# A decoder block on one core: the first modulation columns summed two at a time, the first loads reordered, the rotary tables ahead, and the combinations of h as a stream

## The chip, the cores and the metric

The kernel runs on one core of a Trainium2 chip. The time is the device time of one execution, in microseconds; the kernel before takes 2710.49 us, the median of three runs from 2708.99 to 2712.02. PE is the matrix engine, DVE the vector engine, ACT the scalar engine, POOL GpSimd and SP the engine that issues most loads.

## The reference

One decoder block: 2048 tokens, 1024 features, float32 throughout. The parts that the change touches:

```python
mod = c @ w_ada[l] + b_ada[l]
shift_m, scale_m, gate_m, shift_f, scale_f, gate_f = jnp.split(mod, 6, axis=-1)

h = modulate(rms_norm(x, g_pre_mix[l]), shift_m, scale_m)      # h * (1 + scale) + shift
proj = h @ w_in[l]
q_a, k_a, v_a, q_m, k_m, v_m, o_m, i_m, f_m, g_a, g_m = jnp.split(proj, split_points, axis=-1)

q_a = rope(q_a.reshape(B, S, N_Q_HEADS, HEAD_DIM), positions)   # sin and cos of positions * inv_freq
k_a = rope(k_a.reshape(B, S, N_KV_HEADS, HEAD_DIM), positions)
...
```

Behind it come sliding-window attention with sinks, a chunkwise mLSTM, a gated merge with its output projection, and a SwiGLU feed-forward part. The modulation `mod` is a vector of 6 x 1024 numbers, the same for all tokens: no projection can start before the shift and scale of its columns of h are known.

## The kernel before

Every float32 matrix is split into a rounded high half and the rest, a low half (`whi` and `wlo` for weights, `hi` and `lo` for h). A product is three matmuls into one sum: high by high, high by low, low by high. ACT rounds the high halves (L256, L259, L518) and a subtraction gives the low ones (L257 and L260 for weights, L521 for h).

Tokens go in four blocks of 512 (`TB`), two blocks to a super-block of 1024 (`T2`). Within one, the q, k, v and mLSTM v projections of the first block come first, then those of the second, then projections that use both blocks at once with fewer products: they need `hcT1` to `hcT4`, combinations of h's blocks. `hprep` makes h of one block: loads of x, sums of squares on ACT (L500), the reciprocal root on POOL (L475), the scaled rows, then for each of 8 columns k (128 features each) a transposition on PE (L209) and two activations with that column's scale and shift (L518 the rounded half, L520 the full value), and the low half (L521, on POOL in the first block, on DVE in the others). In the odd block it also makes the combinations (L534 to L537) as soon as columns k and k+4 are there. `hsums` then moves two of the combinations within memory and splits them (L551, L552).

The start. `ADA` cuts the first 1024 shift and the first 1024 scale columns of `w_ada` into four chunks of 256. `load_ada` brings one chunk, 2 MB in four loads of 512 KB (L129). `ada_first` multiplies the 8 row groups of a chunk by c and adds them up, shift and scale each in an accumulator of its own, 128x256 per operation (L426 the first, L428 the other seven), on DVE. The shift of chunk 0 is summed on PE instead (16 matmuls, L204, then a copy on ACT, L443). Matmuls with ones add over the partitions, and L448 to L450 write the columns of `sh1` and `s1` for two k at a time; `first_h` then steps `hprep` through these two columns. `rope_tables` (L631 to L679) reduces position times frequency to an angle in some 35 operations on DVE and takes sine and cosine on ACT. `program()` puts it before the fourth chunk.

The order on each engine comes from a planner: it simulates the program and picks what can be issued next, so that the place of an instruction in the text does not fix its place in an engine's queue, except where a call pins it (`tc.issue_after`, `tc.keep_in_program_order`). Streams (`spawn`) are stepped as the planned time of PE, `now`, passes their due time, which a generator yields as a delay (`L_HT`, `L_HS` and others, ns). Loads of weights go through `wpool`'s raw tiles: a load waits until both halves of what was in its buffer are made. The first raw tiles hold the q weights (`raw_rows`, L290), then k, v and the gates' (`raw_cols`), then the mLSTM v weights (L290 again).

Of the kernel before, what the change touches and what calls it, by code (L numbers as in the profile page):

```python
# [10 lines left out]
F32 = mybir.dt.float32  # L11
F32R = mybir.dt.float32r
I32 = mybir.dt.int32
# [6 lines left out]
P = 128  # L20
# [17 lines left out]

L_X, L_HT, L_HS = 16000.0, 1400.0, 1500.0
L_ROPE, L_ROPEK, L_QK, L_ATT2 = 5000.0, 2100.0, 1500.0, 3500.0  # L40
# [8 lines left out]

ADA = [(0, 256, (0,)), (256, 256, ()), (512, 256, ()), (768, 256, ())]  # L50
ADA_AHEAD = (1, 3, 4)

# [19 lines left out]
def decoder_block(ctx: ExitStack, tc: tile.TileContext, a: dict, out: bass.AP, dbg=None):  # L72
# [48 lines left out]
    def load_ada(c0, n):  # L121

        kn = 2048 // n
        raws = {0: [], 1: []}
        for k0 in range(0, KD, 4):
            for part in (0, 1):
                if k0 % kn == 0:
                    raws[part].append(big([kn, n]))
                nc.sync.dma_start(raws[part][-1][:, k0 % kn:k0 % kn + 4, :],  # L129
                                  w_ada[:, part * D + c0:part * D + c0 + n].rearrange("(p k) c -> p k c", k=KD)[:, k0:k0 + 4, :])  # L130
        return {part: [raws[part][k // kn][:, k % kn, :] for k in range(KD)] for part in (0, 1)}

    x_first = [load_x(x_d, big, 0)]

    stack = tm([P, P])
    V.memset(stack, 0.0)
    r0 = 0
    off = {}
    for name, v, n in (("b_ada", a["b_ada"].rearrange("o (t p) -> (o t) p", p=P), 48),
                       ("g_pre_mix", a["g_pre_mix"].rearrange("o (t p) -> (o t) p", p=P), 8),  # L140
                       ("g_pre_ffn", a["g_pre_ffn"].rearrange("o (t p) -> (o t) p", p=P), 8),
                       ("conv_w", a["conv_w"].rearrange("o j (t p) -> (o j t) p", p=P), 32),
                       ("conv_b", a["conv_b"].rearrange("o (t p) -> (o t) p", p=P), 8),
                       ("norm_w", a["mlstm_norm_w"].rearrange("o (t p) -> (o t) p", p=P), 4)):
        nc.sync.dma_start(stack[r0:r0 + n, :], v)
        off[name] = r0
        r0 += n
    x_first.append(load_x(x_d, big, 1))
    posi = tm([S // P, P], I32)
    nc.sync.dma_start(posi, a["positions"].rearrange("o (t p) -> (o t) p", p=P))  # L150
    c_sb = const.tile([P, KD], F32, name="c_sb")
    nc.sync.dma_start(c_sb, a["c"].rearrange("o (p k) -> (o p) k", k=KD))
# [127 lines left out]
    def raw_cols(w, nk, c0, n):  # L280
# [4 lines left out]
        return Raw(load)  # L285

    def raw_rows(w, k0, nk, c0):
        def load():
            t = raw_tile([nk, 512])
            nc.sync.dma_start(t, w[k0 * P:(k0 + nk) * P, c0:c0 + 512].rearrange("(k p) c -> p k c", p=P))  # L290
            return t
        return Raw(load)
# [136 lines left out]

    def ada_first(c0, n, raws, on_pe):  # L430

        t0, nt = c0 // P, n // P
        acc = [tm([P, n]) for _ in range(2)]
        pt = mix_tile()
        ps = {part: mix_tile() for part in on_pe}
        for k in range(KD):
            for part in (0, 1):
                if part in on_pe:
                    mm(ps[part][0:1, :n], c_sb[:, k:k + 1], raws[part][k], k == 0, k == KD - 1)
                else:  # L440
                    ada_terms(acc[part], raws[part][k].unsqueeze(1), k, 1)
        for part in on_pe:
            A.copy(acc[part][0:1, :], ps[part][0:1, :n])  # L443
        for part in (0, 1):
            r = 1 if part in on_pe else P
            for j in range(nt):
                mm(pt[:, part * 8 + j:part * 8 + j + 1], acc[part][:r, j * P:(j + 1) * P], ones[:r, 0:1], True, True)
        V.tensor_tensor(sh1[:, t0:t0 + nt], pt[:, :nt], col("b_ada", t0, nt), op=ALU.add)  # L448
        V.tensor_tensor(s1[:, t0:t0 + nt], pt[:, 8:8 + nt], b1[:, 8 + t0:8 + t0 + nt], op=ALU.add)
        V.tensor_tensor(s1[:, t0:t0 + nt], s1[:, t0:t0 + nt], col("g_pre_mix", t0, nt), op=ALU.mult)  # L450

# [34 lines left out]
    def hprep(b, first=False):  # L486
# [25 lines left out]
        def one(k):  # L512
            name = f"{k // 4 + 1}{odd + 1}"
            hi, lo = (hc_part(name, i)[:, k % 4, :] for i in range(2))
            ps = mix_tile()
            for t in range(NT):
                transpose(ps[:, t * P:(t + 1) * P], xs[t][:, k * P:(k + 1) * P])
            A.activation(hi, ps, AF.Identity, scale=s1[:, k:k + 1], bias=sh1[:, k:k + 1])  # L518
            v = vs[k // 4][:, k % 4, :]
            A.activation(v, ps, AF.Identity, scale=s1[:, k:k + 1], bias=sh1[:, k:k + 1])  # L520
            (G if first else V).tensor_tensor(lo, v, hi.bitcast(F32), op=ALU.subtract)  # L521

# [100 lines left out]
    NS = T2 // P  # L623

    def rope_tables(sb):

# [47 lines left out]
        V.tensor_scalar(y, y, -lim, lim, op0=ALU.max, op1=ALU.min)  # L674
        V.scalar_tensor_tensor(t2, y, -1.0, y, op0=ALU.mult, op1=ALU.min)
        sin = small.tile([P, NS, 32], F32, tag="sin", name=nm("sin"), bufs=1)
# [34 lines left out]
    def c_tile(n):  # L711
        C[n] = kvp.tile([P, MH, MD + 1], F32, tag="cst", name=nm("cst"), bufs=3)
        return C[n]

    hp0 = hprep(0, first=True)
    next(hp0)
    tables = {}

    def first_h(c0, n, on_pe):
        ada_first(c0, n, ada_raws[c0], on_pe)  # L720
        for _ in range(n // P):
            next(hp0)
# [13 lines left out]
    def superblock(sb):  # L736
# [1101 lines left out]
    phase2 = run2(program2())  # L1838
    for _ in run2(program(), {i: lambda i=i: ada_raws.update({c0: load_ada(c0, n) for c0, n, _ in ADA[ADA_AHEAD[i - 1]:ADA_AHEAD[i]]}) for i in (1, 2)}):
        pass  # L1840
# [29 lines left out]
```

## Time and profile before

| | |
|---|---|
| runs | 2708.99, 2710.49, 2712.02 us |
| the profiled execution's own time | 2716.59 us |
| its span, first to last instruction | 2714.9 us |
| mean granted clock of PE | 0.990 |
| HBM traffic over the span | 185 GB/s |
| low halves of the first h on POOL (L521) | 8, 1.45 us mean |
| chunk sums on DVE up to 62 us (L426, L428) | 56, 28.1 us busy |

The page gives busy times and shares for each engine; a group line gives the line of the code, the engine, the operation, what is written and read, how often, and the busy time, mean length and idle time before it with what ended that. A line of the timeline begins with the start in us from the span's start, and the length; `x4` means that four equal instructions run one behind another and overlap; in square brackets stands how long the engine had been idle and what it waited for. SPq is SP's queue, where the length is that of issuing a load and not of its transfer.

### The profile page before, as it was taken

The numbers are of one execution on the slowest core, as the hardware profiler recorded it, in microseconds if no ns is written. First come the engines' busy times: TensorE is split into PE (matmuls) and PEld (weight loads), VectorE is DVE, ScalarE is ACT, GpSimd is POOL, SyncE is SP. The second block draws the span as 40 slices with busy tenths as digits, with TensorE's granted clock in tenths as the row PEclk, the third lists the DMA queues.
The fourth block names the chain that finished last, engine by engine and source line by source line (L and its number), as shares of the span: only waits on it lengthen the run. The fifth ranks groups of instructions, "written<-read, shape, count | busy, mean of one in ns | idle before, by whom it ended". The sixth has DMA issues, their size and how long they took to land.

```text
span 2714.9 us, 35793 instructions
## 1 busy us (share of the span) xinstructions
PE 2639.2 (97%) x12310; PEld 2138.9 (79%) x12310; DVE 1986.2 (73%) x3906; ACT 1299.8 (48%) x2558; POOL 148.2 (5%) x189
## 2 busy tenths in 40 slices
PE   6989999999998999999999999999999999999998
PEld 4867788888885678888887888888877888888886
DVE  7968788778695778876687777776677676766456
ACT  5556544444755564444563443335554333333444
POOL 2010001100101000110000000000000000000000
PEclk8999999999998999999999999999999999999999
DMA  7654355897574544678765564436675232324566
GB/s 249 206 184 157 128 172 179 269 340 248 196 235 147 196 138 138 213 231 291 251 224 198 175 201 152 155 113 213 215 271 188 97 117 86 113 97 144 186 210 217
DMA packets 353639, 511.90 MB, mean 189 GB/s; under 512 B 25120, under 2 KB 213660, under 8 KB 348208
## 3 DMA queue, kind: packets, MB, share of 16 engines
q1 hardware_dynamic: 353456, 509.61, 56.9%
q8 instruction: 97, 1.59, 0.2%
q14 instruction: 86, 0.70, 0.1%
HBM read 357.12 MB, written 144.02 MB: 185 GB/s over the span
## 4 chain that ended last, share of the span: by engine, by line
PE 85%; DVE 7%; DMA 4%; ACT 2%; issue 1%; POOL 0%; SPq 0%; DVEq 0%; ACTq 0%; POOLq 0%
PE acc L204 61%; PE mix L204 22%; PE mix L209 2%; DVE hl L1357 1%; DVE tm L428 1%; DMA raw<-as_d 1%; ACT tm L946 1%; ACT hl L1356 1%; DMA raw<-in_w_in_dram 1%; DMA at_d<-tx 0%; DMA big<-in_x_dram 0%; DVE wlo L260 0%; DMA tx<-in_w_ada_dram 0%; DVE w L1667 0%; DMA at<-at_d 0%
## 5 line engine op out<-in xcount | busy, mean ns | idle before, releaser
L204 PE MATMUL acc<-big,hl 128*128 128x512 f32 x3936 | 940.8, 394 | 4.3 <-ACT tx L827 1.8
L204 PEld LDWEIGHTS acc<-big,hl 128*128 128x128 f32 x3936 | 733.3, 188 | 172.5 <-issue 13.8
L1356 ACT CAST hl<-raw 128x512 fp32r<-128x512 f32 x732 | 440.1, 621 | 493.4 <-PE acc L204 222.2
L1357 DVE TENSOR_TENSOR hl<-raw,hl 128x512 fp32r<-128x512 f32 x732 | 496.3, 694 | 194.8 <-ACT hl L1356 194.0
L204 PE MATMUL acc<-whi,big 128*128 128x512 f32 (+1 forms) x1280 | 379.3, 377 | 10.8 <-ACT big L518 8.4
L204 PEld LDWEIGHTS acc<-whi,big 128*128 128x128 f32 x1280 | 236.2, 192 | 52.4 <-ACT big L518 8.5
L204 PE MATMUL mix<-big,hl 128*128 128x512 f32 x1056 | 263.9, 391 | 1.7 <-ACT hl L1356 1.1
L204 PE MATMUL acc<-wlo,big 128*128 128x512 f32 (+1 forms) x640 | 241.2, 379 | 6.4 <-DVE wlo L260 6.4
L204 PE MATMUL acc<-hl,hl 128*128 128x512 f32 x1008 | 237.4, 393 | 5.1 <-DVE hl L1357 3.4
L204 PEld LDWEIGHTS mix<-big,hl 128*128 128x128 f32 x1056 | 197.9, 188 | 45.9 <-ACT hl L1356 1.9
L204 PEld LDWEIGHTS acc<-hl,hl 128*128 128x128 f32 x1008 | 187.0, 188 | 50.9 <-DVE hl L1357 8.8
L204 PE MATMUL mix<-hl,hl 128*128 128x512 f32 x792 | 182.7, 391 | 1.3 <-DVE hl L1357 0.9
L204 PEld LDWEIGHTS mix<-hl,hl 128*128 128x128 f32 x792 | 147.9, 188 | 35.3 <-DVE hl L1357 3.1
L204 PE MATMUL acc<-big,whi 128*128 128x512 f32 x512 | 157.4, 393 | 0.0
L260 DVE TENSOR_TENSOR wlo<-raw,whi 128x1024 fp32r<-128x1024 f32 (+1 forms) x96 | 109.0, 1137 | 65.5 <-ACT whi L259 59.8
L259 ACT CAST whi<-raw 128x1024 fp32r<-128x1024 f32 (+1 forms) x96 | 94.3, 983 | 123.8 <-PE acc L204 110.4
L204 PEld LDWEIGHTS acc<-wlo,big 128*128 128x128 f32 x640 | 123.7, 193 | 28.3 <-DVE wlo L260 8.6
L475 POOL TENSOR_TENSOR rs<-ms,nhalf 128x1 f32<-128x1 f32 (+1 forms) x56 | 42.6, 772 | 1617.5 <-DVE ms L473 1610.5
L204 PE MATMUL mix<-hcT4h,hl 128*128 128x512 f32 x352 | 117.7, 395 | 0.7 <-ACT hl L1356 0.7
L204 PE MATMUL acc<-hcT2h,hl 128*128 128x512 f32 x352 | 117.6, 394 | 0.0
L204 PEld LDWEIGHTS acc<-big,whi 128*128 128x128 f32 x512 | 95.4, 188 | 19.2
L204 PE MATMUL acc<-big,wlo 128*128 128x512 f32 x256 | 97.7, 393 | 0.0
(330 smaller groups left out, 3491.5 us busy)
## 6 DMA issues: line engine op xcount, KB each, us to landing
raw<-in_w_in_dram SPq DMA_DIRECT2D x48, 1024.0 KB
as_d<-w SPq DMA_DIRECT2D x154, 256.0 KB
raw<-as_d SPq DMA_DIRECT2D x70, 512.0 KB
raw<-in_w_ffn_gate_dram SPq DMA_DIRECT2D x22, 1024.0 KB
raw<-in_w_ffn_up_dram SPq DMA_DIRECT2D x22, 1024.0 KB
raw<-ws_d SPq DMA_DIRECT2D x40, 512.0 KB
y_d<-tm SPq DMA_DIRECT2D x64, 256.0 KB
tx<-in_w_ada_dram SPq DMA_DIRECT2D x64, 256.0 KB
```

The source lines that it names most:

```text
L204: T.matmul(o, lhsT=lhsT, rhs=rhs, start=start, stop=stop, skip_group_check=resumed)
L209: T.transpose(o, i, ident[:k, :k])
L259: A.copy(hv, src)
L260: V.tensor_tensor(lv, src, hv.bitcast(F32), op=ALU.subtract)
L428: V.scalar_tensor_tensor(acc, raw[:, k, :], c_, acc, op0=ALU.mult, op1=ALU.add)
L475: G.tensor_tensor(r[:, :n], ms[:, :n], nhalf[:, :n], op=ALU.pow)
L946: A.activation(sc[g][:, j, :], sc[g][:, j, :], AF.Exp, bias=nm_[:, hd:hd + 1], accum_out=sums[:, hd:hd + 1])
L1356: A.copy(v(hi), src)
L1357: V.tensor_tensor(v(lo), src, v(hi).bitcast(F32), op=ALU.subtract)
```

## The change

Six things change, all in the first phase:

- `load_ada` puts shift and scale of a chunk into one tile side by side, still in four loads. `ada_first` becomes `ada_half` (four of the eight row groups of a chunk; one operation of 128x512 sums both) and `ada_columns` (the matmuls with ones, and one operation for each column of `s1` and `sh1`, 16 and not 12 in all). Nothing of it is left on PE but the matmuls with ones. `first_h(i)` issues the first half of chunk i+1 ahead of the columns of chunk i, and its second half behind them.
- `last_sum` pins the first sum of each chunk behind the last sum of the chunk before; for chunk 0 behind the last operation of `rope_tables(0)`, which is called before the first chunk.
- First loads: x0, positions, c, x1, the first q weights, then the chunks (the loads of the first two q weights are kept in the program's order). The eight small vectors load through ACT's queue.
- The low halves of the first h (L521) are subtracted on DVE.
- The combinations leave `hprep` for a stream of their own, `hcombos`, with two steps for each k, spawned with a delay of 12000, which then goes on to `hsums` of T2 and T4.
- `ADA_AHEAD` becomes (0, 3, 4): none of the chunks is loaded ahead of the planned program.

```diff
-ADA = [(0, 256, (0,)), (256, 256, ()), (512, 256, ()), (768, 256, ())]
-ADA_AHEAD = (1, 3, 4)
+ADA = [(0, 256), (256, 256), (512, 256), (768, 256)]
+ADA_AHEAD = (0, 3, 4)
...
+        raws = []
+        src = w_ada[:, :2 * D].rearrange("(p k) (s c) -> p k s c", k=KD, s=2)
         for k0 in range(0, KD, 4):
+            raw = big([4, 2 * n]).rearrange("p k (s c) -> p k s c", s=2)
+            for s_ in range(2):
+                nc.sync.dma_start(raw[:, :, s_, :], src[:, k0:k0 + 4, s_, c0:c0 + n])
+            raws += [raw[:, k, :, :] for k in range(4)]
+        return raws
-    x_first = [load_x(x_d, big, 0)]
...
+    posi = tm([S // P, P], I32)
+    nc.sync.dma_start(posi, a["positions"].rearrange("o (t p) -> (o t) p", p=P))
+    x_first = [load_x(x_d, big, 0)]
+    c_sb = const.tile([P, KD], F32, name="c_sb")
+    nc.sync.dma_start(c_sb, a["c"].rearrange("o (p k) -> (o p) k", k=KD))
+    x_first.append(load_x(x_d, big, 1))
...
-        nc.sync.dma_start(stack[r0:r0 + n, :], v)
+        nc.scalar.dma_start(stack[r0:r0 + n, :], v)
...
-    nc.sync.dma_start(b_if, a["b_if"].to_broadcast([P, 8]))
+    nc.scalar.dma_start(b_if, a["b_if"].to_broadcast([P, 8]))
...
-    nc.sync.dma_start(sinks, a["attn_sinks"].to_broadcast([P, HQ]))
-    ada_raws = {c0: load_ada(c0, n) for c0, n, _ in ADA[:ADA_AHEAD[0]]}
+    nc.scalar.dma_start(sinks, a["attn_sinks"].to_broadcast([P, HQ]))
...
+            ins = nc.sync.dma_start(t, w[k0 * P:(k0 + nk) * P, c0:c0 + 512].rearrange("(k p) c -> p k c", p=P))
+            if first_rows:
+                tc.keep_in_program_order(ins)
+                first_rows.pop()
...
-    def ada_first(c0, n, raws, on_pe):
...
+    def ada_half(c0, n, raws, half):
+        if half == 0:
+            ada_acc[c0] = tm([P, 2, n])
+        acc = ada_acc[c0]
+        for k in range(4 * half, 4 * half + 4):
+            c_ = c_sb[:, k:k + 1]
+            if k == 0:
+                with tc.issue_after(last_sum[0].ins):
+                    last_sum[0] = V.tensor_scalar(acc, raws[k], c_, None, op0=ALU.mult)
+            else:
+                last_sum[0] = V.scalar_tensor_tensor(acc, raws[k], c_, acc, op0=ALU.mult, op1=ALU.add)
+                if k == 4:
+                    tc.keep_in_program_order(last_sum[0])
+
+    def ada_columns(c0, n):
         t0, nt = c0 // P, n // P
+        acc = ada_acc[c0]
         pt = mix_tile()
+        for part in (1, 0):
             for j in range(nt):
+                mm(pt[:, part * 8 + j:part * 8 + j + 1], acc[:, part, j * P:(j + 1) * P], ones[:, 0:1], True, True)
+        for j in range(nt):
+            t = t0 + j
+            V.scalar_tensor_tensor(s1[:, t:t + 1], pt[:, 8 + j:9 + j], b1[:, 8 + t:9 + t], col("g_pre_mix", t), op0=ALU.add, op1=ALU.mult)
+            V.tensor_tensor(sh1[:, t:t + 1], pt[:, j:j + 1], col("b_ada", t), op=ALU.add)
...
-            (G if first else V).tensor_tensor(lo, v, hi.bitcast(F32), op=ALU.subtract)
+            V.tensor_tensor(lo, v, hi.bitcast(F32), op=ALU.subtract)
...
+    def hcombos():
+        for k in range(4):
             t1, t2, t3, t4 = (HR[n][:, k, :] for n in ("T1", "T2", "T3", "T4"))
             V.tensor_tensor(t1, t3, t1, op=ALU.subtract)
             V.tensor_tensor(t3, t2, t3, op=ALU.subtract)
+            yield L_HS
             V.tensor_tensor(t2, t2, t1, op=ALU.subtract)
             V.tensor_tensor(t4, t4, t2, op=ALU.subtract)
-            yield L_HT
+            yield L_HS
+        yield from hsums(("T2", "T4"))
...
-        V.scalar_tensor_tensor(t2, y, -1.0, y, op0=ALU.mult, op1=ALU.min)
+        last_sum[0] = V.scalar_tensor_tensor(t2, y, -1.0, y, op0=ALU.mult, op1=ALU.min)
...
+    tables[0] = rope_tables(0)
+
+    def first_h(i):
+        def half(j, h):
+            if j < len(ADA):
+                ada_half(*ADA[j], ada_raws[ADA[j][0]], h)
+        if i == 0:
+            half(0, 0)
+            half(0, 1)
+        half(i + 1, 0)
+        ada_columns(*ADA[i])
+        half(i + 1, 1)
+        for _ in range(ADA[i][1] // P):
             next(hp0)
...
-        yield lambda: hps.update(t=spawn(hsums(("T2", "T4"))))
+        yield lambda: hps.update(t=spawn(hcombos(), L_HCB))
...
-        for i, ch in enumerate(ADA):
-            if i == 3:
-                yield lambda: tables.update({0: rope_tables(0)})
-            yield lambda ch=ch: first_h(*ch)
+        for i in range(len(ADA)):
+            yield lambda i=i: first_h(i)
```

More of the change, by code (lines that the diff above doesn't have):

```diff
@@ L428, in ada_terms @@
                 V.scalar_tensor_tensor(acc, raw[:, k, :], c_, acc, op0=ALU.mult, op1=ALU.add)
-    def ada_first(c0, n, raws, on_pe):
+    ada_acc = {}
+    def ada_half(c0, n, raws, half):
[12 more added lines that the diff above has]
+    def ada_columns(c0, n):
         t0, nt = c0 // P, n // P
-        acc = [tm([P, n]) for _ in range(2)]
+        acc = ada_acc[c0]
         pt = mix_tile()
[L435 to L445, printed above, removed]
-            for j in range(nt):
[L447 to L450, printed above, removed]
+        for part in (1, 0):
+            for j in range(nt):
+                mm(pt[:, part * 8 + j:part * 8 + j + 1], acc[:, part, j * P:(j + 1) * P], ones[:, 0:1], True, True)
[3 more added lines that the diff above has]
+            V.tensor_tensor(sh1[:, t:t + 1], pt[:, j:j + 1], col("b_ada", t), op=ALU.add)
     def ada_stream(parts, gap):
@@ L1838, in decoder_block @@
     phase2 = run2(program2())
[L1839 removed]
+    for _ in run2(program(), {i: lambda i=i: ada_raws.update({c0: load_ada(c0, n) for c0, n in ADA[ADA_AHEAD[i - 1]:ADA_AHEAD[i]]}) for i in (1, 2)}):
         pass
```

24 lines of the change are left out of this document (5 added, 19 removed).

## The prediction

> **What bounds the kernel now.** I read the page first, then a table of stretches with each engine's busy time, then the timeline of the first 80 us.
>
> ```profile
> span 2714.9 us, 35793 instructions
> PE 2639.2 (97%) x12310; PEld 2138.9 (79%) x12310; DVE 1986.2 (73%) x3906; ACT 1299.8 (48%) x2558; POOL 148.2 (5%) x189
> ...
> 0.00:20.00 20.00, 6.69 (x18) 2.13 (x18) 9.51 (x39) 10.50 (x21) 3.97 (x45) 1.00 0.79 281
> 20.00:40.00 20.00, 12.65 (x56) 10.18 (x56) 19.93 (x53) 6.59 (x12) 2.81 (x2) 0.81 1.08 388
> 40.00:60.00 20.00, 15.79 (x78) 13.16 (x79) 15.88 (x40) 11.40 (x18) 7.33 (x5) 0.85 0.36 126
> 60.00:80.00 20.00, 17.46 (x117) 15.40 (x117) 16.52 (x37) 16.44 (x37) 3.29 (x5) 1.00 0.23 79
> ...
> 100.00:120.00 20.00, 17.95 (x106) 16.02 (x106) 16.67 (x42) 11.15 (x22) 0.00 (x0) 0.94 0.91 301
> ...
> 160.00:180.00 20.00, 13.14 (x80) 8.03 (x79) 10.63 (x31) 13.11 (x48) 4.16 (x4) 0.89 0.43 138
> ...
> 200.00:740.00 540.00, 539.97 (x2595) 439.99 (x2594) 418.42 (x881) 294.15 (x591) 50.92 (x51) 1.00 0.65 213
> 740.00:1000.00 260.00, 240.01 (x1236) 182.36 (x1234) 200.62 (x506) 145.59 (x363) 17.52 (x17) 0.95 0.57 182
> ```
>
> Behind a stretch and its length come the busy us of PE, PE's weight loads, DVE, ACT and POOL, then granted clock, DMA share and GB/s. PE is busy 97% of the span and does not pause between 200 and 740 us, so a delay of PE's work before 200 us arrives at 740 us whole. PE is idle for 27.4 us of the first 80 (80 less 6.69, 12.65, 15.79, 17.46), 2.05 us in 100 to 120, 6.86 us in 160 to 180. From 20 to 40 us DVE is the full engine (19.93 of 20): PE waits for the modulation's sums.
>
> ```profile
> 6.03 0.63 ACT L500 ACTIVATE big<-big 128x512 f32<-128x512 f32 x1 [3.96 <-DMA big<-in_x_dram]
> 9.85 0.43 DVE L631 TENSOR_TENSOR tx<-inv_freq,pos 128x256 f32<-128x256 f32 x1
> 10.62 0.61 ACT L500 ACTIVATE big<-big 128x512 f32<-128x512 f32 x1
> ...
> 13.95 5.96 PE L204 MATMUL mix<-big,c_sb 128*1 128x256 f32 x16 [4.43 <-DMA big<-in_w_ada_dram]
> 15.33 0.35 DVE L426 TENSOR_SCALAR tm<-big,c_sb 128x256 f32<-128x256 f32 x1 [3.41 <-DMA big<-in_w_ada_dram]
> ...
> 25.26 0.15 DVE L450 TENSOR_TENSOR s<-s,cols 128x2 f32<-128x2 f32 x1
> 26.34 0.80 PE L204 MATMUL acc<-whi,big 128*128 128x512 f32 x1 [3.79 <-ACT big L518]
> 27.18 2.94 DVE L428 SCALAR_TENSOR_TENSOR tm<-big,c_sb,tm 128x256 f32<-128x256 f32 x2
> ...
> 35.20 1.67 DVE L428 SCALAR_TENSOR_TENSOR tm<-big,c_sb,tm 128x256 f32<-128x256 f32 x4
> 44.47 3.33 DVE L428 SCALAR_TENSOR_TENSOR tm<-big,c_sb,tm 128x256 f32<-128x256 f32 x3
> 52.09 0.42 DVE L675 SCALAR_TENSOR_TENSOR tx<-tx 128x256 f32<-128x256 f32 x1
> 54.90 0.16 DVE L450 TENSOR_TENSOR s<-s,cols 128x2 f32<-128x2 f32 x1
> ```
>
> The rotary table (L631 to L675) runs from 9.85 to 52.09, slipped between the modulation's sums, and for 3.41 us before 15.33 DVE has nothing but the coming of w_ada. The scale of chunk 0 is ready at 25.26, PE's first product follows at 26.34, and the scale of chunk 3 is ready at 54.90.
>
> **The change part by part.** The built program's order shows the rest alike: PE's order differs only in about the first 300 us and in a stretch of super-block 1 near 740 to 1000 us.
>
> *First loads.* The eight small loads leave SP's queue for ACT's, and stand there ahead of ACT's table load and first Squares. There are eight completion lanes for the two queues together: ACT's sixth load waits for the landing of positions, which SP issues right behind x0, and its last for that of c.
>
> ```profile
> 1.29 0.45 SPq L145 DMA_DIRECT2D tm<-in_b_ada_dram  x1
> 0.79 1.28 ACT L500 ACT_TABLE_LOAD   x1 [0.79 <-PEq L1860]
> 7.79 3.15 SPq L129 DMA_DIRECT2D big<-in_w_ada_dram  x4
> ```
>
> An issue takes some 0.45 us. x0 was there at 6.03; two or three issues after that (about 1.2 us) and the table load (1.28 us, formerly hidden behind x0's coming) put the first Square at about 8.5. Eight Squares took from 6.03 to 11.4 (the last starts at 10.62, with 0.8 to its reading); without the wait for x1 they take 5.0, to 13.5. The sum of squares stands ahead of the rotary table in DVE's order, so the table begins at about 13.9 instead of 9.85: +4.05. Bounds: 11.5, if ACT isn't held at all (the Squares then end as before), and 14.5. w_ada comes some 3 us sooner (SP issued it first at 7.79, behind x0's landing), and nobody uses that, since DVE is busy with the table.
>
> *Table ahead, one wide sum.* A pin puts every sum of chunk 0 behind the table's last operation.
>
> ```profile
> L668 DVE SCALAR_TENSOR_TENSOR tx<-tx,tx 128x256 f32<-128x256 f32 x6 | 2.5, 417 | 0.0
> ...
> 11.31 0.29 DVE L639 TENSOR_SCALAR tx<-tx 128x256 f32<-128x256 f32 x1
> 11.63 0.29 DVE L640 TENSOR_SCALAR tx<-tx 128x256 f32<-128x256 f32 x1
> ...
> L428 DVE SCALAR_TENSOR_TENSOR tm<-tx,c_sb,tm x56: 653/746/1542, 319.7 to 1129.8; 128x512 f32<-128x512 f32 x56
> L426 DVE TENSOR_SCALAR tm<-tx,c_sb 128x512 f32<-128x512 f32 x8 | 3.8, 478 | 0.6 <-DMA tx<-in_w_ada_dram 0.6
> L521 DVE TENSOR_TENSOR big<-big,big 128x512 fp32r<-128x512 f32 x24 | 16.4, 688 | 8.5 <-ACT big L520 5.8 <-DMA x1n<-tm 2.4
> ```
>
> The table is 35 operations, 19 of the 0.417 kind and 16 of the 0.29 kind: 12.6 us. Each needs the one before, which costs 0.03 us between neighbours (11.31 to 11.63 for 0.29), so 13.6; four low halves of weights among them, 0.69 long like L521's but overlapping, add about 2.2, and the table ends at 13.9 + 15.8 = 29.7. A chunk's sum is then 0.48 + 7 x 0.775 (median 0.746 + 0.03) = 5.9 us. Before it was 16 operations of 0.40 (1.67 for four, less the last one's tail), 6.4, or 8 of them for chunk 0, whose shift PE summed in idle time (5.96 us at 13.95). One operation twice as wide thus saves 0.02 us a row, not half: independent narrow ones overlap by 0.08, a chain of wide ones pays 0.03. I take 0.775; the bounds are 0.653 and 0.85.
>
> [...]
>
> Chunk 0's scale needs its sum and the next chunk's first three rows: 29.7 + 5.9 + 2.0 + 0.4 = 38.0, where it was 25.26. Chunk 3's: 29.7 + 4 x 5.9 + six low parts of h x 0.65 + four low halves of weights x 0.65 + 1.7 for 16 narrow sums and tails = 61.5, where it was 54.90. Those +6.6 are +4.05 for the start, +3.9 for the low parts that come from POOL (0.688 each), about +3.9 for a table without overlap, +1.2 for the sums, +1.3 for two low halves that had come later, less 3.4 for the wait for w_ada, less 4.1 for operations that POOL's subtractions held up (2.94 for two at 27.18 and 3.33 for three at 44.47, where 0.9 and 1.3 are usual).
>
> *What is late next.* The second group of x rows loads on SP behind a transfer that waits for DVE.
>
> ```profile
> 37.10 3.22 SPq L118 DMA_DIRECT2D big<-in_x_dram  x2
> 56.92 1.98 DVE L257 TENSOR_TENSOR wlo<-raw,whi 128x512 fp32r<-128x512 f32 x2 [1.86 <-ACT whi L256]
> 57.29 0.80 ACT L518 ACTIVATE big<-mix,sh,s 128x512 fp32r<-128x512 f32 x1
> 58.83 2.63 POOL L521 TENSOR_TENSOR big<-big,big 128x512 fp32r<-128x512 f32 x2 [1.08 <-ACT big L520]
> 58.93 0.37 SPq L290 DMA_DIRECT2D raw<-in_w_in_dram  x1
> 59.95 0.66 ACT L500 ACTIVATE big<-big 128x512 f32<-128x512 f32 x1
> 66.58 0.39 PE L204 MATMUL acc<-whi,big 128*128 128x264 f32 x1
> 68.29 0.42 DVE L757 TENSOR_TENSOR tx<-tx,sin 128x256 f32<-128x256 f32 x1
> 78.47 0.70 DVE L260 TENSOR_TENSOR wlo<-raw,whi 128x528 fp32r<-128x528 f32 x1
> ```
>
> Before, x2 and x3 went out at 37.10, ahead of the weights at 58.93 that need the buffer which the low halves at 56.92 release. Now these weights stand ahead of x2 and x3, and they wait for the same low halves, at about 55.8. At 388 GB/s 1 MB takes 2.7 us, and I add 2 us to the landing, an estimate from x0, whose 1 MB took 5.2 us from the start of the queues at 0.79 to its use at 6.03, beside other loads: x2 is there at 55.8 + 2 + 2 x 2.7 = 63.2, x3 at 65.9. In ACT's order x2's Squares stand ahead of the activations of columns 6 and 7 of h, which are thus held until 65.7 (57.29 before), four Squares after 63.2. PE's q products end at about 72.8 and its k and v products start at 74.3 instead of 66.58 (+7.7): less than 8.4, since POOL's slow last subtraction is gone. DVE's rotation starts at about 73.7 (68.29, +5.4), and combinations of h now stand ahead of the third piece of the k and v weights: 88.2 against 78.47 (+9.7). PE's 2.05 us of idle at 100 to 120 take up part of it. I carry +8.
>
> *Combinations.* The later stream moves 16 subtractions of 0.6 us (super-block 0), but in the built order of DVE they come no later than before; I give this part nothing, with 3 us either way for PE's 6.86 us idle at 160 to 180, and 3 either way for super-block 1, where 20 us are idle between 740 and 1000.
>
> **Sum.** The profiled execution's own time was 2716.6 us, 1.7 more than its span of 2714.9, and 6.1 over the median of 2710.5. On its own time the sum gives 2724.6, on the median 2718.5, 0.3% slower.
>
> **Rivals.**
> *Much slower.* The delay grows where DVE is full: if combinations ahead of each weight piece keep DVE 9.7 to 10.2 us late and the idle at 160 to 180 grows by 3, the sum is +13: 2724. For it: 20 to 40 us is full and DVE has no slack to catch up; against it: DVE's 16.52 of 20 at 60 to 80 leaves some.
> *No change.* x2 doesn't hold ACT: the weights' wait ends sooner, or x2 lands by 59. Then columns 6 and 7 follow chunk 3's scale, +6.6, less 2.6 for POOL's last subtraction (58.83), less 2.05 of idle taken up, less up to 2.4 if the table starts at its bound: about 0, 2710.5. For it: 23 us lay between x2's issue at 37.10 and its use at 59.95, so that a landing may be quicker than I add up.
> *Faster.* DVE hides the fixed part of an instruction in a dependent chain as it does between independent ones. The 35 operations of the table then save 0.11 us each (0.08 of overlap gained, 0.03 of gap gone), 3.9, and the 28 sums run at the minimum of 0.653, saving 28 x 0.122 = 3.4. Chunk 3's scale comes at 54.2, 0.7 before its old time; x2 lands near 56, in time; without POOL's last 2.6 PE is 3.3 us early: 2707, and 2705 with the table's start at its bound. It decides once the table ends before 26 us. For it: the minimum of 0.653 occurred; against it: the median of 56 is 0.746. [...]
>
> **How the numbers follow.** Some 0.2% (5.4 us) is what a measurement of this kernel can tell from no change. Chances: my forecast 0.53, much slower 0.13, no change 0.15, faster 0.19, of which 0.14 goes beyond 0.2%. The likeliest's own range is 2713 to 2725: 2.4 down and 0.6 up for the start, 3 each way for the attention and for super-block 1, not all at once. To leave out no more than two in ten I go from 2704 to 2729. Slower by over 0.2%: 0.53 + 0.13 = 0.66; within it 0.15 + 0.05 = 0.20; faster 0.14.
>
> **What would show it.** The first rotary operation at 13.9 (wrong if under 11.5); first PE product near 39 and chunk 3's scale near 61.5; wide sums at 0.775 apart; the Square of x2 at 63 with columns 6 and 7 behind it; k and v products from 74. If the k and v products start before 67, the forecast has the wrong sign. If PE's idle time at 160 to 180 or at 740 to 1000 moves by over 5 us, the combinations do what I gave nothing for.

## The result and the profile after

The kernel after takes 2725.99 us (median of 6 runs, 2724.76 to 2734.15), the kernel before beside it 2712.01 (6 runs, 2708.99 to 2714.57): a ratio of 1.0058, 95% interval 1.0044 to 1.0073, so 12 to 20 us slower. The forecast of 2718.5 had the sign and most of the chain of causes; the loss is nearly twice its 8 us.

The table of stretches of the kernel after, with the columns as in the prediction:

```profile
0.00:20.00 20.00, 0.66 (x2) 0.36 (x2) 6.83 (x30) 10.48 (x23) 3.82 (x45) 1.00 0.88 318
20.00:40.00 20.00, 1.99 (x10) 1.99 (x11) 18.70 (x42) 4.24 (x6) 0.00 (x0) 1.00 1.05 369
40.00:60.00 20.00, 18.15 (x88) 14.96 (x87) 17.98 (x38) 8.27 (x13) 0.00 (x0) 1.00 0.01 1
60.00:80.00 20.00, 17.13 (x96) 14.31 (x97) 12.25 (x27) 14.88 (x32) 1.87 (x3) 1.00 0.42 158
80.00:140.00 60.00, 55.09 (x366) 49.61 (x365) 53.48 (x144) 34.67 (x63) 0.00 (x0) 0.94 0.68 222
...
200.00:740.00 540.00, 538.04 (x2597) 439.29 (x2596) 420.60 (x890) 287.25 (x575) 45.36 (x45) 1.00 0.64 213
```

PE does 2.65 us of work in the first 40 us (0.66 + 1.99), where the kernel before did 19.34, and is nearly as full as before between 200 and 740 (538.04 us, where it was 539.97). From 40 to 60 us the loads that were sent have landed (1 GB/s); DVE, full before, has 17.98 of 20, and PE 18.15. From 80 to 140 us PE is idle for 4.91 us; in the kernel before it was 2.05:

```profile
80.00:140.00 60.00, 57.95 (x353) 51.11 (x353) 54.72 (x175) 36.09 (x81) 1.69 (x2) 0.97 0.76 240
```

The timeline of the kernel after, in order of time:

```profile
2.35 0.29 ACTq L149 DMA_DIRECT2D tm<-in_g_pre_ffn_dram  x1
7.97 0.32 ACTq L149 DMA_DIRECT2D tm<-in_conv_w_dram  x1
9.51 1.28 ACT L509 ACT_TABLE_LOAD   x1 [9.51 <-DMA tm<-in_mlstm_norm_w_dram]
10.81 0.63 ACT L509 ACTIVATE big<-big 128x512 f32<-128x512 f32 x1
16.09 0.42 DVE L647 TENSOR_TENSOR tx<-inv_freq,pos 128x256 f32<-128x256 f32 x1
31.42 0.42 DVE L691 SCALAR_TENSOR_TENSOR tx<-tx 128x256 f32<-128x256 f32 x1
31.96 0.49 DVE L443 TENSOR_SCALAR tm<-big,c_sb 128x512 f32<-128x512 f32 x1
32.48 5.48 DVE L445 SCALAR_TENSOR_TENSOR tm<-big,c_sb,tm 128x512 f32<-128x512 f32 x7
38.01 1.86 PE L202 MATMUL mix<-ones,tm 128*128 128x1 f32 x8 [23.62 <-DVE tm L445]
40.12 0.21 DVE L458 SCALAR_TENSOR_TENSOR s<-mix,b,cols 128x1 f32<-128x1 f32 x1
41.70 0.80 PE L202 MATMUL acc<-whi,big 128*128 128x512 f32 x1
44.34 0.75 DVE L445 SCALAR_TENSOR_TENSOR tm<-big,c_sb,tm 128x512 f32<-128x512 f32 x1
48.83 0.95 PE L202 MATMUL mix<-ones,tm 128*128 128x1 f32 x8
50.49 0.21 DVE L458 SCALAR_TENSOR_TENSOR s<-mix,b,cols 128x1 f32<-128x1 f32 x1
59.41 0.21 DVE L458 SCALAR_TENSOR_TENSOR s<-mix,b,cols 128x1 f32<-128x1 f32 x1
...
67.04 0.63 ACT L509 ACTIVATE big<-big 128x512 f32<-128x512 f32 x1 [1.09 <-DMA big<-in_x_dram]
67.17 0.21 DVE L458 SCALAR_TENSOR_TENSOR s<-mix,b,cols 128x1 f32<-128x1 f32 x1
69.51 0.76 ACT L527 ACTIVATE big<-mix,sh,s 128x512 fp32r<-128x512 f32 x1
70.32 0.50 PE L202 MATMUL acc<-whi,big 128*128 128x512 f32 x1 [2.46 <-ACT big L527]
78.04 0.36 PE L202 MATMUL acc<-whi,big 128*128 128x264 f32 x1
...
92.59 0.59 PE L202 MATMUL acc<-wlo,big 128*128 128x264 f32 x1 [3.07 <-DVE wlo L258]
```

Five readings. ACT stands between its fourth load (2.35) and its fifth (7.97), so that the first Square comes at 10.81 and the table starts at 16.09. The table ends at 31.84, chunk 0's sum takes from 31.96 to 37.96, and PE has waited 23.62 us for it. Once PE has work, the scales are 10.4, 8.9 and 7.8 us apart (40.12, 50.49, 59.41, 67.17): the sum of chunk 1 ends at 45.1 (its last row starts at 44.34), but its matmuls with ones (48.83) stand on PE behind the products of chunk 0, which began at 41.70. The sums of chunks 2 and 3 end at 54.8 and 63.8, and their matmuls with ones start at 57.1 and 66.0, again behind products. Next, the Square of x2 (67.04) stands ahead of column 6 (69.51), whose scale was there at 67.3; PE waits 2.46 us. Last, at 92.59 PE waits 3.07 us for the low half of the third piece of the k and v weights.

To follow a delay through the span I take one marker: the last Square of block 3's x, near 715 us, behind all that the change reorders in super-block 0 and ahead of super-block 1's reordered part. In the rows below, behind the shortest, median and longest time in ns, stand the starts of the first and of the last of the 32 Squares: the last is the marker.

```profile
L500 ACT ACTIVATE big<-big x32: 612/618/661, 6.0 to 715.9; 128x512 f32<-128x512 f32 x32
```

```profile
L509 ACT ACTIVATE big<-big x32: 612/617/634, 10.8 to 729.4; 128x512 f32<-128x512 f32 x32
```

The first is the kernel before, the second the kernel after: 13.5 us late at the marker. That is about the whole loss (the spans differ by 14.0); behind the marker the trace of the kernel after first gains 3.6 us, up to 969 us, and then loses 4.1.

### The profile page after: what moved, and what is told of

Same layout as the page of the kernel before. It is cut to its first block, busy times and chain, and to the rows that moved or that the text cites. A ratio compares the mean times of both kernels' runs of the same rounds, so it can differ in the third digit from the quotient of the medians.

```text
span 2728.9 us, 35725 instructions
## 1 busy us (share of the span) xinstructions
PE 2636.4 (97%) x12294; PEld 2136.2 (78%) x12294; DVE 1987.3 (73%) x3894; ACT 1300.4 (48%) x2557; POOL 135.8 (5%) x181
## 4 chain that ended last, share of the span: by engine, by line
PE 82%; DVE 6%; DMA 5%; ACT 3%; issue 2%; POOL 0%; SPq 0%; ACTq 0%; DVEq 0%; POOLq 0%
PE acc L202 57%; PE mix L202 23%; PE mix L207 2%; DVE hl L1383 1%; DMA at_d<-tx 1%; ACT tm L972 1%; DMA raw<-ws_d 1%; ACT hl L1382 1%; DMA raw<-as_d 1%; DMA raw<-in_w_in_dram 1%; DMA big<-in_x_dram 0%; DMA tx<-in_w_ada_dram 0%; ACT big L509 0%; DMA at<-at_d 0%; DVE wlo L258 0%
```

## The experiments

Each run was compared with the kernel before on the same chip (medians there of 2710.0 to 2712.4). In short:

| kernel | time, us | k and v products start, us | marker, us |
|---|---|---|---|
| before | 2712.0 | 66.6 | 715.9 |
| after | 2726.0 | 78.0 | 729.4 |
| e1 after, table among the sums | 2717.8 | 70.2 | 721.1 |
| e2 after, small loads on SP | 2724.6 | 74.3 | 726.0 |
| e3 after, combinations back | 2730.1 | 77.8 | 730.5 |
| e4 before, with the stream | 2724.4 | 66.3 | 716.5 |
| e5 before again | 2708.1 (one run) | 66.2 | 714.5 |
| e6 after, e1 and e2 together | 2720.4 | 73.7 | 718.5 |
| e7 after, x2 and x3 early | 2729.3 | 78.0 | 724.6 |
| e8 after, low halves on POOL | 2732.0 | 78.3 | 729.1 |
| e9 before, with the table ahead | 2724.3 | 74.9 | 729.3 |
| e10 after, two narrow sums | 2729.9 | 77.7 | 730.5 |
| e11 before, first chunk sooner | 2722.4 | 69.6 | 722.4 |
| e12 before, low halves on DVE | 2709.7 | 65.5 | 717.7 |

The start of the k and v products and the marker are read from one trace of each kernel. They don't move alike: e6, e7 and e9 gain or lose 3 to 5 us between the two.

### e5: what one execution can tell

> The kernel before once more, unchanged, for a second trace: it tells which differences of a few us between the traces belong to the kernel and which to one execution. Theory: up to 700 us the two traces of the kernel before agree within 1 us, so that the lag of 13.5 us of the kernel after at 700 us is the change's; what differs between 740 and 1000 and behind 1400 us may be the execution's. Rival (the start of the first trace was an unusual one): the two differ by 3 us or more before 200 us.

The marker and the last masking of the attention (L933), in the first trace of the kernel before and in this one:

```profile
L933 DVE COPY_PREDICATED tm<-m_prev,mix x60: 411/442/452, 129.1 to 969.4; 128x256 f32<-128x256 uint32 x60
```

```profile
L500 ACT ACTIVATE big<-big x32: 612/618/663, 5.9 to 714.5; 128x512 f32<-128x512 f32 x32
L933 DVE COPY_PREDICATED tm<-m_prev,mix x60: 413/441/452, 128.9 to 961.3; 128x256 f32<-128x256 uint32 x60
```

Up to the marker the two executions of one program differ by 1.4 us, between it and 969 us by 6.7 more (8.1 less 1.4), and by 0.4 in the rest. By this one pair the marker is good to some 1.5 us and a whole trace to 8. The gain of 3.6 us that the first two traces seemed to show for the kernel after in super-block 1 (13.5 late at the marker, 9.9 at 969) is within what one execution does by itself; against the second trace of before it would be a loss of 3.1. From the marker to the last masking all traces of this case take 244.9 to 254.4 us, the kernels with the stream of combinations no less than those without. The gain is dropped.

### e1 and e9: the table ahead

e1 puts the table among the sums again:

```diff
-    tables[0] = rope_tables(0)
...
-                with tc.issue_after(last_sum[0].ins):
+                with tc.issue_after(last_sum[0].ins) if last_sum[0] else ExitStack():
...
+            if i == 3:
+                yield lambda: tables.update({0: rope_tables(0)})
```

> The kernel after, but the rotary table of super-block 0 is called before the fourth chunk again and no sum waits for it. Theory (the pinned table is most of the loss): the first product stood at 41.7 us against 26.3 before, of which the table's own 15 us of DVE are what the pin adds; chunk 0's sum can start when w_ada has landed, near 14, so the first product comes at 25 to 29 us and the time falls by 10 to 13 us, to 2713 to 2716. Rival (the late first Squares and the chain from chunk to chunk on PE set the start, whatever DVE does first): the first product stays beyond 36 us and the time falls by less than 4.

```profile
17.48 0.48 DVE L443 TENSOR_SCALAR tm<-big,c_sb 128x512 f32<-128x512 f32 x1
29.52 0.22 DVE L458 SCALAR_TENSOR_TENSOR s<-mix,b,cols 128x1 f32<-128x1 f32 x1
30.73 0.79 PE L202 MATMUL acc<-whi,big 128*128 128x512 f32 x1 [0.19 <-ACT big L527]
L509 ACT ACTIVATE big<-big x32: 612/616/632, 10.5 to 721.1; 128x512 f32<-128x512 f32 x32
```

In the timeline and the marker's row of e1 the first sum starts at 17.48 in place of 31.96, the first product comes 11.0 us sooner (30.73, where I expected 25 to 29), the k and v products 7.8, and 8.3 us arrive at the marker. The time is 2717.79 (ratio to before 1.0026, 1.0015 to 1.0037), 8.2 us under the kernel after: less than the 10 to 13 that I expected, twice the rival's bound. The table ahead is the largest part of the loss.

e9 adds the table ahead to the kernel before, with its narrow sums, its PE sum and its loads:

```diff
+    tables[0] = rope_tables(0)
...
-                    ada_terms(acc[part], raws[part][k].unsqueeze(1), k, 1)
+                    with tc.issue_after(last_sum[0].ins) if k == 0 else ExitStack():
+                        done = ada_terms(acc[part], raws[part][k].unsqueeze(1), k, 1)
+        last_sum[0] = done
```

> The kernel before with one thing added: the rotary table is called before the first chunk, the first sums wait for its last operation and each chunk's first sums for the last sum of the chunk before, as in the kernel after; two narrow accumulators, chunk 0's shift on PE, the loads and the rest as before. Theory (the pinned table is the main loss and needs nothing else of the change): the table runs from 9.8 to about 26, the scale of chunk 0 is ready at 32 to 34 where it was 25.3, the lag at 715 us is 6 to 9 us and the time 2718 to 2721. Rival (without the later start of the table PE's idle time takes it up): the lag at 715 us is under 3 us.

The timeline of e9 on POOL, PE and DVE:

```profile
36.83 9.97 POOL L524 TENSOR_TENSOR big<-big,big 128x512 fp32r<-128x512 f32 x2 [22.83 <-ACT big L523]
39.22 5.23 DVE L428 SCALAR_TENSOR_TENSOR tm<-big,c_sb,tm 128x256 f32<-128x256 f32 x13
45.62 1.22 PE L204 MATMUL acc<-whi,big 128*128 128x512 f32 x2 [5.70 <-POOL big L524]
51.94 0.16 DVE L451 TENSOR_TENSOR sh<-mix,cols 128x2 f32<-128x2 f32 x1 [7.49 <-PE mix L204]
```

The scale of chunk 0 is ready at 35.2, close to what was expected. But the marker stands at 729.3 and the time at 2724.30, as late as with the whole change and beyond the 6 to 9 us expected. The sums, no longer mixed with the table, run without a gap (13 in 5.23 us), and the two subtractions on POOL beside them take 9.97 us where 2.63 to 3.6 are usual; PE waits 5.70 us for them, and DVE 7.49 for the matmuls with ones behind. So the table ahead costs the kernel before about 13.4 us by itself, and undoing it gives the kernel after 8.3: its price depends on the rest. The wait on POOL is a part of the 13.4. The k and v products start 8.3 us late in e9; where the other 5.1 us up to the marker are lost is not shown. In the kernel after the wait on POOL does not occur, and e8 shows that this isn't owed to DVE's taking the subtractions: with them on POOL they take 1.28 to 1.82 us there.

### e2 and e6: the small loads

```diff
-        nc.scalar.dma_start(stack[r0:r0 + n, :], v)
+        nc.sync.dma_start(stack[r0:r0 + n, :], v)
...
-    nc.scalar.dma_start(b_if, a["b_if"].to_broadcast([P, 8]))
+    nc.sync.dma_start(b_if, a["b_if"].to_broadcast([P, 8]))
```

and the same for the sinks; e6 makes e1's edit as well.

> The kernel after, but the eight small loads are issued on SP again, behind x1 and ahead of the first weights. Theory (ACT stood waiting in its own queue of loads): the first Square goes back from 10.8 us to 6 to 7, the table starts 4 to 5 us sooner, and the time falls by 3.5 to 5 us, to 2721 to 2722.5. Rival (the small loads on SP push w_ada back by 3 us, and what was gained at the table is lost there, or PE's chain takes it): the time stays within 1.5 us of the kernel after.

> The kernel after with both undone: the rotary table among the sums, and the small loads on SP. Theory (both delays are of the same start and add up, since the first product waits for one chain of DVE): the first product comes 4 us sooner than with the table alone (30.3), at 25 to 27 us, and the time falls below 2714, 4 us under the table alone (2717.8). Rival (the loads of w_ada then set the start, which the small loads push back): within 1.5 us of the table alone.

```profile
L509 ACT ACTIVATE big<-big x32: 612/616/632, 5.7 to 726.0; 128x512 f32<-128x512 f32 x32
```

```profile
L509 ACT ACTIVATE big<-big x32: 612/616/633, 5.8 to 718.5; 128x512 f32<-128x512 f32 x32
18.92 0.49 DVE L443 TENSOR_SCALAR tm<-big,c_sb 128x512 f32<-128x512 f32 x1 [0.96 <-DMA big<-in_w_ada_dram]
31.27 0.80 PE L202 MATMUL acc<-whi,big 128*128 128x512 f32 x1
```

The first row is e2's, the other three are e6's. With the loads on SP the first Square is at 5.7 (6.0 before). In e2 the table starts at 11.20, 4.9 us sooner, the k and v products 3.7 and the marker 3.4. e6 missed its forecast: its first product comes at 31.27, not at 25 to 27, and no sooner than e1's 30.73, because its first sum waits until 18.92 for w_ada (17.48 in e1). That is the rival's condition: with the small loads on SP, w_ada comes later. Its k and v products start 3.5 us behind e1's. Its marker is yet 2.6 us ahead of e1's, so this gain arises between 74 and 715 us, and I can't name its place. That 8.3 and 3.4 us alone make nearly the 10.9 together is thus no proof that the two delays add up; at the start they don't. Nor do the times show it: e2 is 1.4 us under the kernel after (2724.62), which is the rival's outcome, and e6 at 2720.41 is above e1. The times take in the part behind the marker, which one execution moves by 7 us, so the traces are read here up to the marker only.

### e7: x2 and x3 early

```diff
-        xbs = x_first if first else [load_x
+        xbs = x_first if first else x_second if b == 1 else [load_x
...
+        if i == 0:
+            x_second.extend(load_x(x_d[TB:2 * TB, :], big, j) for j in range(2))
```

> The kernel after, but the second group of x rows (x2, x3) is loaded behind the last chunk of w_ada and ahead of the k, v and mLSTM v weights. Theory (the second term of the prediction: x2 came at 67.0 and its Squares held columns 6 and 7 until 69.5, 2.3 us beyond their scale at 67.3): columns 6 and 7 follow their scale directly, the k and v products start 2 to 3 us sooner (75 to 76 for 78.0), and the time falls by 1 to 3 us, to 2723 to 2725. Rival (ACT's hold was hidden behind PE's products of the third chunk): no change of the k and v products' start.

```profile
67.94 0.78 ACT L528 ACTIVATE big<-mix,sh,s 128x512 fp32r<-128x512 f32 x1
77.36 0.60 ACT L810 COPY tx<-acc 128x512 f32<-128x512 f32 x1
78.00 0.39 PE L202 MATMUL acc<-whi,big 128*128 128x264 f32 x1 [2.10 <-ACT tx L810]
```

Column 6 comes 1.6 us sooner (67.94 for 69.51), as expected, but the k and v products start where they did (78.00 for 78.04): PE now waits 2.10 us for ACT's evacuation of the q products (77.36), which stands behind the first columns of the next block that the early x2 and x3 brought forward (from 74.69). That is the rival's outcome, but by another way: the edit made a new hold. The marker is yet 4.8 us sooner (724.6), so something behind 78 us gains, and its place is open; the time is 3.3 us longer (2729.30). What the hold of x2 costs in the kernel after isn't shown by this.

### e8 and e12: the low halves

e8 puts the subtraction in the kernel after on POOL, e12 puts it in the kernel before on DVE:

```diff
-            V.tensor_tensor(lo, v, hi.bitcast(F32), op=ALU.subtract)
+            (G if first else V).tensor_tensor(lo, v, hi.bitcast(F32), op=ALU.subtract)
```

> The kernel after, but the low halves of the first h are subtracted on POOL again. Theory (chunk to chunk PE sets the pace: its products of one chunk, then the matmuls with ones of the next, 8.9 us a chunk, so the 0.69 us of DVE for each low half lie beside PE): the scales come no sooner, POOL's 1.45 us each and the slowed sums cost a little, and the time rises by 0 to 3 us. Rival (DVE's extra 4 us were on the path, as the prediction had them): the scale of chunk 3 comes 3 us sooner and the time falls by 2 to 4 us.

> The kernel before with one part of the change: the low halves of the first h on DVE instead of POOL. A version that may beat both. Theory (the prediction's two terms cancel: 4.1 us of DVE operations held up by POOL go, 8 subtractions of 0.69 us come, and the last one ends 1 us sooner): no DVE sum is longer than 0.6 us, the scale of chunk 3 stays within 1.5 us of 54.9, the lag at 715 us is -1.5 to 1 and the time within 2 us of the kernel before. Rival (DVE is the full engine there, so the added 5 us are on the path): the scale of chunk 3 is 3 us later and the time 3 us or more longer.

The chunk sums of the kernel before and of e12, with their shortest, median and longest time in ns:

```profile
L428 DVE SCALAR_TENSOR_TENSOR tm<-big,c_sb,tm x49: 472/479/1515, 15.9 to 53.0; 128x256 f32<-128x256 f32 x49
```

```profile
L428 DVE SCALAR_TENSOR_TENSOR tm<-big,c_sb,tm x49: 474/478/482, 15.9 to 50.9; 128x256 f32<-128x256 f32 x49
```

In e8 the marker stays (729.1 for 729.4), as theory had it. The scale of chunk 1 comes 1.5 us sooner (48.98 for 50.49), those of chunks 2 and 3 don't (59.54 for 59.41, 67.89 for 67.17), and DVE waits 2.94 us for PE's matmuls with ones of chunk 3. But e8 changes two things, since POOL's subtractions also hold up the sums (four of them take 4.92 us, where 3.1 is usual); the time of 2731.96 is 6 us longer, more than the 3 allowed, and the place behind the marker is open. In e12 no sum is longer than 0.482, where 1.515 occurred, and the last sum starts 2.1 us sooner; the scale of chunk 3 comes at 54.45 (54.90 before). The time is 2709.65 in 11 runs against 2712.42 in 15 (ratio 0.9990, 0.9981 to 0.9999): the only version that came out under both kernels, by 0.3 to 5 us. As one of twelve, with an interval that just leaves out no change, that is weak evidence, and its one trace does not show where: the marker is at 717.7, 1.8 us late where I allowed 1.

### e10: one wide sum or two narrow ones

```diff
-                last_sum[0] = V.scalar_tensor_tensor(acc, raws[k], c_, acc, op0=ALU.mult, op1=ALU.add)
+                for s_ in range(2):
+                    last_sum[0] = V.scalar_tensor_tensor(acc[:, s_, :], raws[k][:, s_, :], c_, acc[:, s_, :], op0=ALU.mult, op1=ALU.add)
```

> The kernel after, but each row group of a chunk is summed by two operations of 128x256, shift and scale apart, in the order of the rows. Theory (a wide operation saves 0.02 us, since narrow ones that don't need each other overlap): chunk 0's sum takes 6.2 to 6.5 us from its first operation to its end, where the wide ones took 6.0 (31.96 to 37.96), and the time stays within 2 us of the kernel after. Rival (each instruction pays a fixed part that a wide one pays once): the sum takes 7.2 us or more.

```profile
31.63 0.35 DVE L443 TENSOR_SCALAR tm<-big,c_sb 128x256 f32<-128x256 f32 x1
...
32.16 5.63 DVE L447 SCALAR_TENSOR_TENSOR tm<-big,c_sb,tm 128x256 f32<-128x256 f32 x14
```

Chunk 0's sum takes 6.16 us with two narrow operations a row (31.63 to 37.79) and 6.0 with one wide one. The change's title part is worth 0.16 us a chunk. The time, 2729.86, is 3.9 us above the kernel after, beyond the 2 us that I allowed, and its place is open: the marker is 1.1 us later, which one execution can do by itself.

### e3 and e4: the stream

e3 moves the combinations back into `hprep`; e4 gives the kernel before the stream `hcombos` with its delay of 12000, and nothing else.

> The kernel after, but the combinations of h are made inside hprep again. Theory (the stream is the one part that gains: the lag fell from 13 to 10 us in super-block 1 between 740 and 1000 us): the lag at 1000 us stays at 13 or 14 and the time rises by 3 to 4 us, to 2729 to 2730; up to 80 us nothing changes. Rival (the combinations ahead of the k and v weights cost what the start doesn't): the time falls by 3 us or more.

> The kernel before with only the combinations moved to the stream with the delay of 12000. Theory: the same gain of 3 to 4 us in super-block 1, and nothing at the start: 2708 to 2709 where the kernel before takes 2712. Rival (the gain comes from PE being late in the kernel after, so that the idle time of super-block 1 is met in another order): no change within 1.5 us, or slower.

e3's marker is at 730.5 (+1.1) and its time 2730.06 (+4.1). That is the size expected, but not at the place: the gain in super-block 1 that it should undo was one execution's, and 1.1 us at the marker is too. e4's marker is at 716.5, 0.6 behind the kernel before, and its time is 2724.43, 12.6 us longer (ratio 1.0045, 1.0027 to 1.0062): my theory was wrong in sign. One place is visible, at the border of the second phase, in e4 and in the kernel before:

```profile
1435.89 0.58 ACT L1502 COPY w<-acc 128x512 f32<-128x512 f32 x1 [5.33 <-DMA x<-tm]
1436.52 0.80 PE L204 MATMUL acc<-hcT2h,hl 128*128 128x512 f32 x1 [2.62 <-ACT w L1502]
```

```profile
1429.03 0.58 ACT L1497 COPY w<-acc 128x512 f32<-128x512 f32 x1
```

In e4 a copy waits 5.33 us for a store to land, and PE for the copy; the same copy in the kernel before does not wait. Here e4 falls 5.4 us further behind, though the change is hundreds of us away. The order on every engine is the same in this stretch, and the store goes out at 1425.78, 1.45 us later than before, as all else there; why the copy waits for it in e4 is open. The spans of these two traces differ by 6.6 us, so the step is most of that. As to the rest of the 12 us, the first trace of the kernel before is itself 4.7 us above the median of the runs beside e4.

### e11: the first chunk sooner

The kernel before with its loads in the order x0, positions, c, chunk 0, x1, small vectors:

```diff
-    ada_raws = {c0: load_ada(c0, n) for c0, n, _ in ADA[:ADA_AHEAD[0]]}
...
+    nc.sync.dma_start(c_sb, a["c"].rearrange("o (p k) -> (o p) k", k=KD))
+    ada_raws = {c0: load_ada(c0, n) for c0, n, _ in ADA[:ADA_AHEAD[0]]}
+    x_first.append(load_x(x_d, big, 1))
```

> The kernel before with another order of the first loads alone: x0, positions, c, chunk 0 of w_ada, x1, then the eight small vectors, all on SP. A version that may beat both: DVE and PE waited 3.4 and 4.4 us for chunk 0, which SP issued first at 7.8. Theory: chunk 0's sums start at 8 to 10 in place of 15.3, the first product comes 2 to 4 us sooner (22 to 24 for 26.3), the lag at 715 us is -1 to -3 and the time 2709 to 2711 where the kernel before takes 2712. Rival (x1 and the small vectors are then late, and the columns wait for b_ada): no gain, first product at 26 or later.

```profile
9.28 0.35 DVE L425 TENSOR_SCALAR tm<-big,c_sb 128x256 f32<-128x256 f32 x1 [0.40 <-DMA big<-in_w_ada_dram]
16.14 0.29 DVE L181 COPY cols<-mix 128x128 f32<-128x128 f32 x1 [2.04 <-PE mix L180]
28.57 0.80 PE L203 MATMUL acc<-whi,big 128*128 128x512 f32 x1 [1.12 <-ACT big L517]
```

The sums start at 9.28, as hoped, but the small vectors are late: their transposition reaches DVE at 16.14, the table starts behind it, and the first product comes at 28.57 (26.34 before). The rival holds: 2722.42 us, 12.4 slower (ratio 1.0044, 1.0031 to 1.0056). What the sums gained by the new order the table lost, since both run on DVE.

## Why the prediction was right, and where its size was off

- *The start: a term that was too small.* ACT's queue of loads held the Squares, as said, but for longer: the table began at 16.09, not 13.9, beyond my bound of 14.5. I took x0's landing from the kernel before. By the semaphore records of the trace eight loads go out by 2.35 on the two queues together, each with a semaphore of its own, and each of the next waits for the load whose semaphore it takes over: the q weights on SP, out at 5.39, for b_if (2.7 us), ACT's fifth load, out at 7.97, for x0, which landed at 7.95, the sixth for positions (8.29), the last for c (8.46). In the kernel before x0 landed at 6.00, and in e2, with the small loads behind it on SP, the Square that reads it starts at 5.7. Four issues on ACT and the table load came behind. The term measured 6.24 and not 4.05. e2 shows the loads on ACT as the cause of 4.9 of it, worth 3.4 us at the marker. w_ada, which I had 3 us sooner, went out at 7.43 (7.79 before).
- *The table ahead.* 15.75 us from 16.09 to 31.84, forecast 15.8. Chunk 0's sum: 6.0, forecast 5.9. Its scale at 40.1, forecast 38.0, all of the difference from the start. The first product at 41.7, forecast near 39. e1 and e9 bear the part out.
- *From chunk to chunk: the step that failed in size.* I spaced the scales by DVE's work and had chunk 3 at 61.5; it came at 67.2. (The parts that I listed for its +6.6 add up to 6.85.) Of these 5.7 us the start explains 2.2. The other 3.5 came because PE, not DVE, set the pace: the sums were ready 3.7, 2.2 and 2.2 us before PE took up their matmuls with ones. Those stand behind the products of the chunk before, 7.1 us of them for chunk 0 (41.70 to 48.83) and 5.6 for the next two, and DVE, ACT and PE then follow in turn. The prediction's "scale of chunk 3" sum had no term of PE. In e8 DVE is spared the low halves, and the scales of chunks 2 and 3 come no sooner.
- *x2.* The 8 of the sum stood on this path: column 6 held until 65.7, 4.2 us behind the scale of chunk 3, and the k and v products 8.6 behind column 6. The path is as described, and later: the weights' load ahead of x2 went out at 59.3 and not 55.8, x2 landed at 67.0 (63.2 forecast) and held column 6 to 69.5, 2.3 us behind its scale, and the k and v products came 8.5 behind that. What the hold is worth is open, since e7 removed it and made another.
- *The sum.* At the start of the k and v products the delay is 11.5 us, not 7.7: the late start and PE's pace. Another 2.0 come up to the marker. There I had let PE's idle time of 2.05 us take up part of the delay; from 80 to 140 us it grew to 4.91, of which 3.07 are the wait for the third weight piece, whose low half I had at 88.2 and which was made at 91.83 (the kernel before has such a wait of 2.1 us).
- *Wide sums.* 0.775 apart was forecast; seven took 5.48 (0.79 apart, at a median of 0.752 each). In e10 sixteen narrow operations take 6.16, the eight wide ones 6.0: 0.16 us a chunk. At the 0.35 and 0.48 that a narrow one takes alone, sixteen end to end would be an estimated 7.4 (2 x 0.35 + 14 x 0.48); in rows they overlap.
- *The rivals.* *Faster* fell with the table's end at 31.84, where it needed 26. The part of an operation that doesn't grow with its width is an estimated 0.21 us by the kernel before (2 x 0.346 at 128x256 less 0.482 at 128x512, L426). In the chains of the kernel after nothing of it was hidden: operations of 0.29 start 0.33 apart (25.45 and 25.78), and the wide sums 0.79. *No change* fell with the late start: nothing took it up, and x2 did hold ACT. *Much slower* had the time (2724), and its wait is there in part: DVE is full from 80 to 100 us, with five combinations between 82 and the weight piece at 91.83. But 11.5 of the 13.5 us stood at 78 us already, and e3, with the combinations back, is no sooner.
- *Combinations.* I gave them nothing. In e3 and e4 they move the marker by 1.1 and 0.6 us, which is within what one execution does. The sign that I named for them did come: PE's idle time went from 6.86 us to none at 160 to 180, and from 20.0 to 14.6 at 740 to 1000. It is no proof of them: from 140 to 200 us the idle time is 6.9 and 6.6, so it only moved, e3 has none at 160 to 180 either, and from 740 to 1000 us the kernels with the stream have less of it (12.7 to 19.9 us, against 17.8 to 22.4) and yet take no less time from the marker to 969 us. What the stream does in the kernel after as a whole stays open; the step of e4 at 1430 us does not occur there.

## What to carry to other kernels

Work that fills the gaps of an engine can cost little; the same work pinned ahead of the chain cost half of its 15.75 us or more here (8.3 at the marker in the kernel after, 13.4 in the kernel before), and in e9, where the sums then ran without a gap, one subtraction on POOL beside them took 8.7 us (2.2 at most in the kernel before). When a late start is summed, add up the engine that becomes full once work arrives, too: the spacing of the chunks was PE's, not DVE's. An edit is not local where a planner decides the order: e7 moved two loads and put other work ahead of ACT's evacuation. Follow more than one marker through the span, and take two traces of the unchanged kernel before reading a few us in a later stage.

## What the runs showed that was not expected

Beside each other, POOL's subtractions grew by much more than DVE's sums did. In e9 one subtraction on POOL took 8.7 us beside back-to-back sums on DVE, where the shortest took 1.27; the longest of all its narrow sums took 1.52, where the median is 0.48:

```profile
L524 POOL TENSOR_TENSOR big<-big,big x8: 1269/1631/8732, 36.8 to 68.9; 128x512 fp32r<-128x512 f32 x8
L428 DVE SCALAR_TENSOR_TENSOR tm<-big,c_sb,tm x49: 469/481/1522, 28.9 to 61.7; 128x256 f32<-128x256 f32 x49
```

In the kernel before, with the table's operations between the sums, POOL's longest was 2.2. In e8, where each wide sum needs the one before, POOL's longest was 1.8, and the sums were stretched instead, to 1.77 at most where 0.75 is the median. With the subtractions on DVE no sum is stretched (0.482 at most in e12, 0.752 in the kernel after). How the two engines come to delay each other is not shown by these runs.

Small loads on a queue of their own were not free for the large load beside them here. x0's 1 MB was issued at 0.79 in the kernel before and at 0.80 in the kernel after. It landed at 6.00 with the small loads on SP, and at 7.95 with them on ACT's queue; in e2, with them on SP again, the Square that reads it starts at 5.7. From 3 to 4 us the transfers moved 426 GB/s in the kernel before and 129 GB/s in the kernel after.
